# Operands of a linear recurrence and of windowed attention: loads that are issued earlier, from a pool of their own

## The chip, the cores and the metric

The kernel runs on one core of a Trainium2 chip as one program. The core has five instruction streams: TensorE (PE, with its weight loads shown as PEld), VectorE (DVE), ScalarE (ACT), GpSimd (POOL) and SyncE (SP, which here does nothing but issue DMAs). The time is that of one execution on the device, in microseconds (us). Of the kernel before there are three timed runs: 4224.21, 4231.0 and 4253.31, median 4231.0. One more execution was profiled.

## The reference, cut to what matters

One inference step of a two-layer backbone over 1280 tokens (256 of a prompt, 1024 latent ones), width 1024, all in float32. Layer 0 mixes by a gated DeltaNet and a short convolution, layer 1 by windowed attention and RWKV-7 side by side; a squared-ReLU MLP follows each. The change is in layer 1:

```python
def rwkv7_mixer(x, rw, s0_f, s0_b):
    x = token_shift_bi(x, mu)
    r, k, v, wl, al, gl = split_cols(x, RWKV_SPLITS)
    w_log = -softplus(-(w0 + einsum(tanh(wl), w_up))) - 0.5      # per direction
    decay = exp(-exp(w_log)); a = sigmoid(a0 + einsum(al, a_up)); gate = sigmoid(gl) @ g_up
    kk = l2norm(k * k_k); k2 = k * (1 + (a - 1) * k_a)
    y2, s2 = vmap(rwkv7_scan)(forward and reversed r, decay, k2, v, kk, a, states)
    y = y2[0] + y2[1][:, ::-1]
    y = groupnorm(y) * ln_w + ln_b
    bonus = sum(r * (k2_fwd + k2_bwd) * r_k) * v                 # over a head
    return (y + bonus) * gate, ...

def odd_mixer_latent(h, w_in, w_out, ...):
    q, k, v, x_rw = odd_project(h, w_in)
    att = attend_latent(rope_2d(q), rope_2d(k), v, ck, cv, sink) # 128-token blocks: 3 local blocks + 512 cached keys
    rwo = rwkv7_mixer(x_rw, rw, ...)
    return concat([att, rwo]) @ w_out
```

RWKV has 8 heads of 64. Two heads fill the 128 partitions, so there are four pairs b, each run in two directions d.

## The kernel before, in words

Every dense product is done in three matmuls: an activation and a weight are each split into a high and a low part (`split`, line 245: the high part by ACT on line 247, the low part by POOL on line 251), and high x high, high x low and low x high are added up in PSUM (line 275 for the projections; line 1283 for those that run later, beside the recurrence). A weight is loaded as `raw` by SP (`load_w`, line 263), then split into `whl`.

The Tile framework chooses each engine's order of instructions ahead of time, by a simulated timeline, and puts semaphores where one engine needs another. On each engine the order is then fixed: an instruction that waits holds up everything behind it, DMA issues on SP's queue included. Buffers come from pools; a tile that takes a place in SBUF over from another has to wait for its last reader.

Layer 1's mixer (`odd_mixer`) runs so:

1. The end of layer 0's MLP, then the norm. Three weight columns are asked for ahead (`ahead`, line 1086). x is written out to DRAM by `spill_x` (line 126).
2. Projections: q, k, v, the low-rank inputs (`sp_l`), and the first pair's r, k, kk (`sp_r`) and v. Results go to DRAM (`sp_...`).
3. The recurrence and attention. Eight units (b, d). `prep` builds a unit's operands in five groups of 256 tokens: loads rkk (line 1550) and lin (line 1553), multiplies lin with the pair's `ups` (loaded on line 1541, used on line 1557), and goes on to the arrays AR, BK and Gm. `recur` runs the unit's recurrence. Beside units 0 and 1 the r, k, v projections of pairs 1 to 3 run (line 1283, weights from a pool of its own). From unit 2 on attention runs beside it: `begin` of a 128-token block loads its keys kS (line 1393), used on line 1426. When both directions of a pair are done, `finish` makes five parts out of it: for each, r and the two k2 rows are loaded into vg (line 1814), added (POOL, line 1816) and multiplied (DVE, line 1817), then v and g are loaded into two of the same three places (lines 1819, 1820), and PE multiplies on lines 1855 and 1860. The last pair's finish is cut in two (`ahead`, lines 1873 and 1874, and `rest`).

Arrays AR of a group live in a pool of 8 buffers, to which `rmore` adds 3 from unit 2 on.

Of the kernel before, what the change touches and what calls it, by code (L numbers as in the profile page):

```python
# [18 lines left out]
P = 128  # L19
# [37 lines left out]
def gram_masks():  # L57

    m = np.zeros((P, 2, 2, P), np.float32)
    j, i = np.arange(64)[:, None], np.arange(64)[None, :]  # L60
    for d in range(2):
        past = (j < i) if d == 0 else (j > i)
        half = np.concatenate([past | (j == i), past], 1)
        m[:, d] = np.concatenate([half, half], 0)[:, None, :]
    return m
# [20 lines left out]
def tile_kernel(ctx, tc, I, O):  # L86
# [996 lines left out]
    def odd_mixer(xt, hs, hes, xes, wes):  # L1083
        wi = I["od_w_in"][0]

        ahead = [load_w(w_cols(wi, 768 + j * P)) for j in (12, 13, 14)]
# [135 lines left out]


# [82 lines left out]
        with ExitStack() as es:  # L1306
            prep, recur, finish = rwkv(es, sp_r, sp_v, sp_t, sp_l, sp_g, sp_k2)
# [21 lines left out]
            for u, (b, d) in enumerate(units):  # L1329
                cur = nxt  # L1330
                start = pace["cum"]
                recur(b, d, cur)
                if u == 2:
                    ed.close()
                    items = attention(es, sp_q, sp_k, sp_c, vtok_dram)
                    state["more"] = pool(es, "rmore", 3)
                if u + 1 < len(units):
                    nxt = prep(*units[u + 1])
                if u < 2:
                    slot, work = work[:per], work[per:]  # L1340
                else:
                    if u == 2:
                        per = iter((26,26,24,24,24, len(items)))
                    n = next(per)
                    slot, items = items[:n], items[n:]
                if u == 7:
                    pre, last = finish(b)
                    slot = [f for k, f in enumerate(slot) for f in ([f, pre.pop(0)] if k % 4 == 3 and pre else [f])] + pre
                    pace["used"] = max(pace["used"], start)
                k0 = len(slot) // 3  # L1350
                for k, f in enumerate(slot):
                    if ends and k >= k0 and (k - k0) * 5 // (len(slot) - k0) > 4 - len(ends):
                        ends.pop(0)()
                    f()
                while ends:
                    ends.pop(0)()
                if d == 1 and b < 3:
                    ends = finish(b)
            for f in last:
                f()  # L1360
        pace["on"] = False

    def attention(es, sp_q, sp_k, sp_c, vtok_dram):
# [145 lines left out]
    def rwkv(es, sp_r, sp_v, sp_t, sp_l, sp_g, sp_k2):  # L1509
# [6 lines left out]
        gmask = rc.tile([P, 2, 2, P], F32, name="gmask")  # L1516
        SY.dma_start(out=gmask, in_=I["cgm"].rearrange("p (d h q) -> p d h q", d=2, h=2))
# [15 lines left out]
        def prep(b, d):  # L1533

            if d == 0:
                ups = tp.tile([P, 3, P], F32, tag="ups", name="ups", bufs=2)
                for i, src in enumerate((I["rwkv_w_up"].rearrange("e d r c -> (e d r) c"),
                                         I["rwkv_a_up"].rearrange("e d r c -> (e d r) c"), I["rwkv_g_up"][0])):  # L1540
                    SY.dma_start(out=ups[:, i], in_=src[:, b * P:(b + 1) * P])
                live["ups", b] = ups
            ups = live["ups", b]
            pc = sp.tile([P, NC], F32, tag="pc", name="pc", bufs=3)
            order = [4, 0, 8, 12, 16] if d == 0 else [16, 0, 12, 8, 4]
            grp = {}
            for c0 in order:
                t0, sl = 64 * c0, slice(64 * c0, 64 * c0 + 256)
                rkk = tp.tile([P, 3, 256], F32, tag="rkk", name="rkk", bufs=2)
                SY.dma_start(out=rkk, in_=sp_r[b][:, :, sl])  # L1550
                r, k, kk = (rkk[:, i].rearrange("p (c q) -> p c q", q=64) for i in range(3))
                lin = tp.tile([P, 2, 256], F32, tag="lin", name="lin", bufs=1)
                SY.dma_start(out=lin[hr[d]], in_=sp_l.rearrange("x p t -> p x t")[hr[d], :, sl])
# [30 lines left out]
                g = state["more"] if state["more"] and turn[0] % 11 in (9, 10, 0) else gp  # L1584
# [9 lines left out]
                for h in range(2):  # L1594
                    ps = ps_t("pp")
                    for c in range(4):
# [3 lines left out]
                                    in1=gmask[:, d, h:h + 1].to_broadcast([P, 4, P]), op=ALU.mult)  # L1600
# [34 lines left out]
        def recur(b, d, unit):  # L1635
# [4 lines left out]
            for s in range(2):  # L1640
                SH[s] = tp.tile([P, 4, 64], F32, tag="SH", name="SH", bufs=4)
                if s == 0:
                    G.memset(SH[s][:, 0], 0.0)
                else:
                    raw = sp.tile([P, 64], F32, tag="sraw", name="sraw", bufs=2)
                    SY.dma_start(out=raw, in_=I[("state_rwkv_fwd", "state_rwkv_bwd")[d]][0, 0, 2 * b:2 * b + 2].rearrange(
                        "h v k -> (h v) k"))
# [158 lines left out]
        def finish(b):  # L1806
# [15 lines left out]
            def head_norm(Yt):  # L1822
# [5 lines left out]
                y2 = tp.tile([P, 4, 64], F32, tag="y2", name="y2", bufs=1)  # L1828
# [17 lines left out]
            def part(c0):  # L1846
                Yt = live.pop(("Y", b, c0 // 4))
                vg = tp.tile([P, 3, 256], F32, tag="vg", name="vg", bufs=1)
                steps = bonus(c0, vg)
                next(steps)  # L1850
                head_norm(Yt)
                next(steps, None)
# [3 lines left out]
                yT = tp.tile([P, 256], F32, tag="yT", name="yT", bufs=1)  # L1856
                affine(yT, ps)
                V.tensor_tensor(out=vg[:, 0], in0=vg[:, 0], in1=ps[:, 256:], op=ALU.mult)
                pg = ps_t("pa")
                PE.matmul(pg[:, :256], ups[:, 2, :], vg[:, 2], start=True, stop=True)  # L1860
                G.tensor_tensor(out=yT, in0=yT, in1=vg[:, 0], op=ALU.add)
# [6 lines left out]
            def ahead(c0):  # L1868
                vg = tp.tile([P, 3, 256], F32, tag="vg", name="vg", bufs=1)
                for _ in bonus(c0, vg):  # L1870
                    pass
                ps = ps_t("pa")
                paced(PE.matmul(ps[:, 256:], C["bd"], vg[:, 1], start=True, stop=True), 0.5)
                paced(PE.matmul(ps[:, :256], ups[:, 2, :], vg[:, 2], start=True, stop=True), 0.5)
                V.tensor_tensor(out=vg[:, 0], in0=vg[:, 0], in1=ps[:, 256:], op=ALU.mult)
# [3 lines left out]
            def rest(c0):  # L1879
# [3 lines left out]
                eg = tp.tile([P, 4, 3, 64] if tg == "BK" else [P, 3, 256], F32, tag=tg, name="eg", bufs=1 if tg == "vg" else 2)  # L1883
# [3 lines left out]
                head_norm(Yt)  # L1887
# [8 lines left out]
            if b < 3:  # L1896
                return [lambda c0=c0: part(c0) for c0 in order]
            return [lambda c0=c0: ahead(c0) for c0 in order], [lambda c0=c0: rest(c0) for c0 in order]
# [127 lines left out]
```

## Time and profile before

| | us |
|---|---|
| three timed runs, median | 4231.0 |
| the profiled execution | 4228.77 |
| its span, from first to last instruction | 4226.4 |
| PE busy | 3917.9 (93%) |
| DVE busy | 2285.1 (54%) |
| POOL busy | 1304.5 (31%) |
| ACT busy | 1287.8 (30%) |
| mean granted TensorE clock | 0.952 |

By the timeline, layer 0's MLP ends at 1860.8, the projections at 2065.1, and the recurrence with attention at 3164. "Idle before" or "waited for" says what released an engine after it had stood idle. [...]

### The profile page before, as it was taken

Reading aid. Unit: us, or ns where it says so; the run is one execution under the profiler, and the core shown is the slowest. Engines: PE = TensorE matmul, PEld = TensorE weight load, DVE = VectorE, ACT = ScalarE, POOL = GpSimd, SP = SyncE. Lnnn points to the kernel's source line nnn. Section 1 sums busy time; section 2 is a strip of 40 time slices with the busy share of each in tenths; the row PEclk is TensorE's granted clock in tenths of the full one; section 3 lists DMA queues with packets and bytes.
Section 4 is the critical chain, followed back from the end, with each engine's and each line's share of the span. In section 5 each row is a group of like instructions: output and inputs, shape, how many; then the busy total and the mean of one; then the engine's idle time right before and its main releaser. Section 6 shows DMA issues by size and latency. Waiting matters only on the chain. (4 is left out here: it accounts for less than half of the span.)

```text
span 4226.4 us, 68798 instructions
## 1 busy us (share of the span) xinstructions
PE 3917.9 (93%) x27295; PEld 3217.3 (76%) x27295; DVE 2285.1 (54%) x4800; ACT 1287.8 (30%) x2728; POOL 1304.5 (31%) x1140
## 2 busy tenths in 40 slices
PE   6989899999999999989889889899769899999999
PEld 4777778787888888878667667677658788888887
DVE  5567656554556665563365567777542533333335
ACT  4454543233111111143222234344231311111112
POOL 3354442233232222333432221322122423232232
PEclk8989999999999999999989799999889999999999
DMA  6333332431222222134565433333242111111111
GB/s 217 90 93 97 92 95 79 139 130 45 65 75 76 75 80 78 56 134 155 159 209 171 131 98 79 90 100 86 58 137 97 30 40 40 41 40 36 35 41 60
DMA packets 438656, 385.52 MB, mean 91 GB/s; under 512 B 125620, under 2 KB 375103, under 8 KB 438207
## 3 DMA queue, kind: packets, MB, share of 16 engines
q1 hardware_dynamic: 410352, 324.88, 26.0%
q10 hardware_dynamic: 27983, 56.24, 4.0%
q8 instruction: 215, 3.52, 0.3%
q14 instruction: 106, 0.87, 0.1%
HBM read 291.62 MB, written 89.39 MB: 90 GB/s over the span
## 5 line engine op out<-in xcount | busy, mean ns | idle before, releaser
L275 PE MATMUL pd<-hhi,whl 128*128 128x512 f32 (+1 forms) x5376 | 1531.9, 364 | 34.8 <-ACT hhi L247 13.5
L275 PEld LDWEIGHTS pd<-hhi,whl 128*128 128x128 f32 x5376 | 973.7, 192 | 195.2 <-ACT hhi L247 14.4
L275 PE MATMUL pd<-hlo,whl 128*128 128x512 f32 (+1 forms) x2688 | 980.2, 365 | 22.8 <-DVE hlo L460 11.8
L517 DVE SCALAR_TENSOR_TENSOR x<-pm,mods,x 128x512 f32<-128x512 f32 (+1 forms) x768 | 503.9, 660 | 720.7 <-PE pm L516 719.3
L251 POOL TENSOR_TENSOR whl<-raw,whl 128x1024 fp32r<-128x1024 f32 (+1 forms) x202 | 472.3, 2349 | 575.0 <-ACT whl L247 575.0
L275 PEld LDWEIGHTS pd<-hlo,whl 128*128 128x128 f32 x2688 | 516.0, 192 | 110.6 <-DVE hlo L460 17.4
L514 PE MATMUL pm<-hh,whl 128*128 128x512 f32 (+1 forms) x1536 | 546.1, 356 | 0.0
L515 PE MATMUL pm<-hl,whl 128*128 128x512 f32 (+1 forms) x1536 | 544.6, 355 | 0.0
L516 PE MATMUL pm<-hh,whl 128*128 128x512 f32 (+1 forms) x1536 | 543.5, 354 | 0.0
L503 ACT ACTIVATE t<-pd 128x512 f32<-128x512 f32 (+1 forms) x192 | 101.3, 528 | 1322.9 <-PE pd L275 1322.9
L251 POOL TENSOR_TENSOR hl<-t,hh 128x512 fp32r<-128x512 f32 (+1 forms) x192 | 216.2, 1127 | 855.3 <-DVE hh L249 855.3
L514 PEld LDWEIGHTS pm<-hh,whl 128*128 128x128 f32 x1536 | 289.1, 188 | 44.3
L515 PEld LDWEIGHTS pm<-hl,whl 128*128 128x128 f32 x1536 | 289.5, 189 | 42.7
L516 PEld LDWEIGHTS pm<-hh,whl 128*128 128x128 f32 x1536 | 289.7, 189 | 42.3
L249 DVE CAST hh<-t 128x512 fp32r<-128x512 f32 (+1 forms) x192 | 134.9, 703 | 193.6 <-ACT t L504 193.6
L247 ACT ACTIVATE whl<-raw 128x1024 fp32r<-128x1024 f32 (+1 forms) x202 | 201.4, 1015 | 124.9 <-PE pm L516 54.2
L366 POOL TENSOR_TENSOR acc<-acc,modw 128x512 f32<-128x512 f32 x112 | 150.5, 1344 | 140.4 <-ACT modw L362 106.6
L354 DVE SCALAR_TENSOR_TENSOR acc<-modw,scp,acc 128x512 f32<-128x512 f32 x168 | 162.9, 969 | 0.0
L362 ACT ACTIVATE modw<-modw,scp 128x256 f32<-128x256 f32 x224 | 112.6, 506 | 86.8 <-DMA modw<-in_mod_w_dram 83.7
L1283 PE MATMUL pa<-hst,whl 128*128 128x512 f32 (+1 forms) x432 | 125.2, 390 | 9.6 <-DMA hst<-sp_h 8.8
L425 ACT ACTIVATE sq<-x 128x512 f32<-128x512 f32 (+1 forms) x120 | 66.2, 559 | 165.4 <-DVE x L1934 49.8
L284 PE MATMUL pd<-hhi,whl 128*128 128x512 f32 (+1 forms) x384 | 109.3, 363 | 2.1 <-DVE xr L1026 1.2
(402 smaller groups left out, 5972.9 us busy)
## 6 DMA issues: line engine op xcount, KB each, us to landing
raw<-in_mlp_w_dram SPq DMA_DIRECT2D x128, 512.0 KB, 3.9
modw<-in_mod_w_dram SPq DMA_DIRECT2D x128, 256.0 KB, 3.0
hst<-sp_h ACTq DMA_DIRECT2D x48, 512.0 KB, 4.4
modw<-in_mod_w_dram SPq DMA_DIRECT2D x128, 128.0 KB, 2.2
rkk<-sp_r SPq DMA_DIRECT2D x40, 384.0 KB, 4.2
raw<-in_ev_w_in_dram SPq DMA_DIRECT2D x28, 512.0 KB, 3.8
x_dram<-x SPq DMA_DIRECT2D x16, 640.0 KB, 6.7
sp_i<-cv SPq DMA_DIRECT2D x12, 640.0 KB, 3.4
```

Of the source, the lines that this page charges most:

```text
L247: A.activation(out=hi, in_=src, func=AF.Copy)
L249: V.tensor_copy(out=hi, in_=src)
L251: G.tensor_tensor(out=lo, in0=src, in1=hi.bitcast(F32), op=ALU.subtract)
L275: paced(PE.matmul(ps[:, :N], w, x[:, t0:t0 + N], start=(n + i == 0), stop=(n == KB - 1 and i == 2)), N / 2400)
L354: bi = V.scalar_tensor_tensor(out=acc[:, s], in0=w, scalar=scp[:, kb, s:s + 1], in1=acc[:, s], op0=ALU.mult, op1=ALU.add)
L362: bi = A.activation(out=dst[:, s], in_=w[:, 0], func=AF.Copy, scale=scp[:, kb, s:s + 1])
L366: G.tensor_tensor(out=acc, in0=acc, in1=w, op=ALU.add)
L514: PE.matmul(ps[:, :N], wh, hh[:, b, :N], start=(b == 0), stop=False)
L515: PE.matmul(ps[:, :N], wh, hl[:, b, :N], start=False, stop=False)
L516: PE.matmul(ps[:, :N], wl, hh[:, b, :N], start=False, stop=(b == 1))
L517: state["evict"] = V.scalar_tensor_tensor(out=xt[db][:, t0:t0 + N], in0=ps[:, :N], scalar=gate[:, db, s:s + 1], in1=xt[db][:, t0:t0 + N], ...
L1283: burst([(lambda w_=w_, i=i, w=w, h=h: PE.matmul(st["ps"][w_][:, :N], st["w"][w_][:, w, kb, :], x[:, h, :N], start=(kb + i == 0), stop=(kb ...
```

## The change

It does six things. (a) At the start of the mixer the weight pools are closed, a pool `rin` is opened, and the weight pools are opened again behind it, at other addresses; ups, rkk and lin live in `rin`, and the first unit's first operands are loaded ahead of the recurrence stage, beside the projections. (b) The mask gmask is halved. (c) The incoming state of a unit is loaded in `prep`, no more in `recur`. (d) Keys kS have two buffers. (e) A finish part has five places in place of three (r, k2, k2, v, g), in a pool of two buffers; all five are loaded together, one part ahead; the separate tiles y2 and yT are gone. (f) `rmore` has 2 buffers in place of 3. No arithmetic changes.

```diff
     def odd_mixer(xt, hs, hes, xes, wes):
+        wes.close()
+        ri = ExitStack()
+        rin = pool(ri, "rin", 1)
+        open_w(wes, 3, 4)
         ahead = [load_w(w_cols(wi, 768 + j * P)) for j in (12, 13, 14)]
...
                     A.dma_start(out=sp_h[kb, :, i], in_=hs[kb][i].bitcast(F32))
+            unit0 = operands(rin, 0, 0, sp_r, sp_l)
...
-                    state["more"] = pool(es, "rmore", 3)
+                    state["more"] = pool(es, "rmore", 2)
+                    state["ends"] = pool(es, "rends", 2)
...
+    def operands(rin, b, d, sp_r, sp_l):
+        hd = slice(64 * d, 64 * d + 64)
+        ups = None
+        if d == 0:
+            ups = rin.tile([P, 3, P], F32, tag="ups", name="ups", bufs=2)
...
+        def group(c0):
+            sl = slice(64 * c0, 64 * c0 + 256)
+            rkk = rin.tile([P, 3, 256], F32, tag="rkk", name="rkk", bufs=2)
+            SY.dma_start(out=rkk, in_=sp_r[b][:, :, sl])
+            lin = rin.tile([P, 2, 256], F32, tag="lin", name="lin", bufs=1)
+            SY.dma_start(out=lin[hd], in_=sp_l.rearrange("x p t -> p x t")[hd, :, sl])
+            return rkk, lin
+        return ups, group, {4: group(4)} if (b, d) == (0, 0) else {}
...
-                kS = ap.tile([P, 4, 3 * P], F32R, tag="kS", name="kS", bufs=1)
+                kS = ap.tile([P, 4, 3 * P], F32R, tag="kS", name="kS", bufs=2)
...
+            raw = sp.tile([P, 64], F32, tag="sraw", name="sraw", bufs=2)
+            SY.dma_start(out=raw, in_=...)            # moved from recur into prep
+            live["raw", b, d] = raw
...
-                g = state["more"] if state["more"] and turn[0] % 11 in (9, 10, 0) else gp
+                g = state["more"] if state["more"] and turn[0] % 10 in (9, 0) else gp
...
-            def bonus(c0, vg):
+            def loads(c0):
                 sl = slice(64 * c0, 64 * c0 + 256)
-                for i, src in enumerate((sp_r[b][:, 0, sl], sp_k2[b % 2, 0][:, sl], sp_k2[b % 2, 1][:, sl])):
+                vg = state["ends"].tile([P, 5, 256], F32, tag="vg", name="vg")
+                for i, src in enumerate((sp_r[b][:, 0, sl], sp_k2[b % 2, 0][:, sl], sp_k2[b % 2, 1][:, sl], sp_v[b][:, sl],
+                                         sp_g[:, sl])):
                     SY.dma_start(out=vg[:, i], in_=src)
-                yield
+                return vg
+            here = {}
+            def operands_of(k):
+                for n in range(k, min(k + 2, 5)):
+                    if n not in here:
+                        here[n] = loads(order[n])
+                return here.pop(k)
+            def bonus(vg):
                 G.tensor_tensor(out=vg[:, 1], in0=vg[:, 1], in1=vg[:, 2], op=ALU.add)
...
-                SY.dma_start(out=vg[:, 0], in_=sp_v[b][:, sl])
-                SY.dma_start(out=vg[:, 2], in_=sp_g[:, sl])
```

How that moves instructions. First SP's queue at the end of layer 0's MLP; `raw<-in_mlp_w_dram` are the MLP's last weights, `raw<-in_od_w_in_dram` the mixer's first, `x_dram<-x` the spills. Before:

```order
L263 DMA raw<-in_mlp_w_dram 128x1024 [waits DMAHW2_49,Pool_49]
L263 DMA raw<-in_od_w_in_dram 128x8x128 [waits DMAHW7_49,DMAHW4_49,Pool_49]
...
L263 DMA raw<-in_od_w_in_dram 128x8x128 [waits DMAHW3_49,DMAHW0_49,Pool_49]
L126 DMA x_dram<-x 128x1280 [waits DVE_49] x5
```

and with the change:

```order
L263 DMA raw<-in_mlp_w_dram 128x1024 [waits DMAHW2_49,Pool_49]
L1378 DMA ups<-in_rwkv_w_up_dram 128x128 [waits DMAHW7_49,DMAHW6_49,Pool_49]
...
L126 DMA x_dram<-x 128x1280 [waits DMAHW1_49,DVE_49]
L263 DMA raw<-in_od_w_in_dram 128x8x128 [waits DMAHW2_49,PE_49]
L263 DMA raw<-in_od_w_in_dram 128x8x128 [waits DMAHW3_49,PE_49]
L263 DMA raw<-in_od_w_in_dram 128x8x128 [waits DMAHW4_49]
L126 DMA x_dram<-x 128x1280 [waits DMAHW5_49,DVE_49]
```

Five loads of the mixer's first weights stood ahead of the spills; now three stand behind the first five spills, and the first two of them wait for PE.

Second, SP's queue where the recurrence stage begins; `sp_k<-k` writes the first group's k2 out and waits for POOL, which makes it. Before:

```order
L263 DMA raw<-in_od_w_in_dram 128x4x128 [waits DMAHW0_49,PE_49]
L1541 DMA ups<-in_rwkv_w_up_dram 128x128 [waits DMAHW2_49,DVE_49,Pool_49]
...
L1550 DMA rkk<-sp_r 128x3x256 [waits DMAHW3_49]
L1553 DMA lin<-sp_l 64x2x256 [waits DMAHW4_49]
L1550 DMA rkk<-sp_r 128x3x256 [waits DMAHW5_49]
L263 DMA raw<-in_od_w_in_dram 128x4x128 [waits DMAHW6_49]
L263 DMA raw<-in_od_w_in_dram 128x4x128 [waits DMAHW7_49,Pool_49]
```

and with the change:

```order
L1571 DMA sraw<-in_state_rwkv_fwd_dram 128x64 [waits DMAHW1_49,PE_49]
L263 DMA raw<-in_od_w_in_dram 128x4x128 [waits DMAHW3_49,PE_49]
L263 DMA raw<-in_od_w_in_dram 128x4x128 [waits DMAHW5_49]
...
L1385 DMA lin<-sp_l 64x2x256 [waits DMAHW3_49,PE_49]
L1607 DMA sp_k_16325<-k_17822 128x256 [waits DMAHW4_49,Pool_49]
L1685 DMA VS<-sp_t 64x4x64 [waits DMAHW5_49]
L263 DMA raw<-in_od_w_in_dram 128x4x128 [waits DMAHW6_49,Pool_49]
```

The first group's operands are gone from this place (they stand among the projections' stores), two weight loads stand at its head, and the third stands behind the store of the first k2.

Third, SP's queue beside unit 2, at the second block's keys and a finish part. Before:

```order
L1819 DMA vg<-sp_v 128x256 [waits DMAHW4_49,DVE_49]
L1820 DMA vg<-sp_g 128x256 [waits DMAHW6_49,DMAHW5_49,Pool_49]
L1550 DMA rkk<-sp_r 128x3x256 [waits DVE_49,Pool_49]
L1393 DMA kS<-sp_k 64x4x384 [waits DMAHW7_49,PE_49]
L1393 DMA kS<-sp_k 64x4x384 [waits DMAHW0_49]
```

and the third block's keys with the change:

```order
L1841 DMA vg<-sp_v 128x256 [waits DMAHW4_49]
L1841 DMA vg<-sp_g 128x256 [waits DMAHW5_49]
L1438 DMA q<-sp_q 64x2x128 [waits DMAHW6_49,PE_49]
L1438 DMA q<-sp_q 64x2x128
L1421 DMA kS<-sp_k 64x4x384 [waits DMAHW0_49]
```

The loads of v and g wait for no arithmetic any more, and from the third block on the keys do not wait for PE to be done with the block before.

## Rows read from the trace of the kernel before

**Rows 1.** Windows: length, each engine's busy time, clock, DMA share, GB/s.
```profile
1860.00:1870.00 10.00, 4.85 (x19) 3.04 (x17) 10.00 (x13) 6.58 (x12) 8.37 (x5) 0.70 1.04 374
1860.00:1900.00 40.00, 27.14 (x99) 19.03 (x98) 29.59 (x47) 23.59 (x42) 18.43 (x20) 0.76 0.68 249
2050.00:2100.00 50.00, 34.99 (x184) 25.84 (x182) 14.01 (x23) 12.03 (x25) 22.69 (x33) 0.83 0.65 197
2100.00:3050.00 950.00, 846.21 (x9485) 648.50 (x9485) 639.50 (x1746) 347.80 (x891) 226.41 (x322) 0.90 0.43 116
```

**Rows 2.** Waits of PE, 2060 to 3180: total us, times, longest.
```profile
PE pa L1426 <- DMA kS<-sp_k: 14.2, 8, 3.1
PE pp L1557 <- DMA lin<-sp_l: 13.0, 1, 13.0
...
PE pa L1873 <- DVE vg L1817: 5.8, 4, 2.2
PE pa L1855 <- DVE vg L1817: 5.7, 3, 4.0
PE pa L1456 <- DVE vg L1858: 5.3, 2, 4.7
...
PE pi L1650 <- DMA sraw<-in_state_rwkv_fwd_dram: 2.1, 1, 2.1
PE pa L1860 <- DVE vg L1858: 2.1, 2, 1.9
...
PE pa L1456 <- DVE yT L1862: 1.2, 1, 1.2
```

**Rows 3.** Timeline of PE, start of the recurrence stage: start, duration, instruction.
```profile
2064.84 0.27 PE L275 MATMUL pd<-hhi,whl 128*128 128x256 f32 x1
2078.13 1.19 PE L1557 MATMUL pp<-lin,ups 64*128 64x256 f32 x2 [13.01 <-DMA lin<-sp_l]
...
2083.96 2.57 PE L1283 MATMUL pa<-hst,whl 128*128 128x512 f32 x6
...
2094.64 0.70 PE L1557 MATMUL pp<-lin,ups 64*128 64x256 f32 x2
```

**Rows 4.** Timeline of SP's issues, same place.
```profile
2064.09 0.38 SPq L263 DMA_DIRECT2D raw<-in_od_w_in_dram  x1
...
2075.50 1.16 SPq L263 DMA_DIRECT2D raw<-in_od_w_in_dram  x2
...
2084.01 1.09 SPq L263 DMA_DIRECT2D raw<-in_od_w_in_dram  x2
2085.20 0.46 SPq L1580 DMA_DIRECT2D sp_k<-k  x1
```

**Rows 5.** DMA issues by what they move: count, KB each, median us to landing.
```profile
x_dram<-x SPq DMA_DIRECT2D x16, 640.0 KB, 6.7
...
raw<-in_od_w_in_dram SPq DMA_DIRECT2D x8, 512.0 KB, 3.9
```

**Rows 6.** Waits of DVE, 2420 to 3060.
```profile
DVE vg L1817 <- POOL vg L1816: 27.4, 11, 5.1
```

**Rows 7.** Waits of POOL, 2420 to 3060.
```profile
POOL vg L1816 <- DMA vg<-sp_k: 35.1, 9, 5.0
POOL AR L1587 <- PE pc L1775: 33.0, 11, 9.3
```

**Rows 8.** Timeline of SP's issues, end of layer 0's MLP.
```profile
1789.89 55.98 SPq L263 DMA_DIRECT2D raw<-in_od_w_in_dram  x5
1855.27 4.28 SPq L126 DMA_DIRECT2D x_dram<-x  x5
```

**Rows 9.** Timeline of PE, first matmul of the projections.
```profile
1860.82 0.39 PE L275 MATMUL pd<-hhi,whl 128*128 128x512 f32 x1
```

**Rows 10.** Timeline of POOL, same norm: a weight's low part, the norm's last low part.
```profile
1862.36 5.14 POOL L251 TENSOR_TENSOR whl<-raw,whl 128x1024 fp32r<-128x1024 f32 x2 [0.16 <-ACT whl L247]
...
1897.60 0.73 POOL L251 TENSOR_TENSOR hlo<-t,hhi 128x256 fp32r<-128x256 f32 x1 [3.42 <-ACT hhi L247]
```

More of the change, by code (lines that the diff above doesn't have):

```diff
@@ L1533, in prep @@
         def prep(b, d):
+            ups, group, first = unit0 if (b, d) == (0, 0) else operands(rin, b, d, sp_r, sp_l)
             if d == 0:
[L1538 to L1541, printed above, removed]
                 live["ups", b] = ups
             ups = live["ups", b]
+            raw = sp.tile([P, 64], F32, tag="sraw", name="sraw", bufs=2)
+            SY.dma_start(out=raw, in_=I[("state_rwkv_fwd", "state_rwkv_bwd")[d]][0, 0, 2 * b:2 * b + 2].rearrange(
+                "h v k -> (h v) k"))
+            live["raw", b, d] = raw
             pc = sp.tile([P, NC], F32, tag="pc", name="pc", bufs=3)
@@ L1548, in prep @@
                 t0, sl = 64 * c0, slice(64 * c0, 64 * c0 + 256)
-                rkk = tp.tile([P, 3, 256], F32, tag="rkk", name="rkk", bufs=2)
-                SY.dma_start(out=rkk, in_=sp_r[b][:, :, sl])
+                rkk, lin = first.pop(c0, None) or group(c0)
                 r, k, kk = (rkk[:, i].rearrange("p (c q) -> p c q", q=64) for i in range(3))
-                lin = tp.tile([P, 2, 256], F32, tag="lin", name="lin", bufs=1)
-                SY.dma_start(out=lin[hr[d]], in_=sp_l.rearrange("x p t -> p x t")[hr[d], :, sl])
                 ps = ps_t("pp")
@@ L1844, in affine, with part @@
                              bias=vec["ln_b"][:, b:b + 1])
-            def part(c0):
+            def part(k):
+                vg = operands_of(k)
+                c0 = order[k]
                 Yt = live.pop(("Y", b, c0 // 4))
[L1848 to L1852, printed above, removed]
+                bonus(vg)
+                head_norm(Yt, vg[:, 2])
                 ps = ps_t("pa")
@@ L1855, in part @@
                 PE.matmul(ps[:, 256:], C["bd"], vg[:, 1], start=True, stop=True)
-                yT = tp.tile([P, 256], F32, tag="yT", name="yT", bufs=1)
+                yT = vg[:, 0]
                 affine(yT, ps)
-                V.tensor_tensor(out=vg[:, 0], in0=vg[:, 0], in1=ps[:, 256:], op=ALU.mult)
+                V.tensor_tensor(out=vg[:, 3], in0=vg[:, 3], in1=ps[:, 256:], op=ALU.mult)
                 pg = ps_t("pa")
-                PE.matmul(pg[:, :256], ups[:, 2, :], vg[:, 2], start=True, stop=True)
-                G.tensor_tensor(out=yT, in0=yT, in1=vg[:, 0], op=ALU.add)
+                PE.matmul(pg[:, :256], ups[:, 2, :], vg[:, 4], start=True, stop=True)
+                G.tensor_tensor(out=yT, in0=yT, in1=vg[:, 3], op=ALU.add)
                 V.tensor_tensor(out=yT, in0=yT, in1=pg[:, :256], op=ALU.mult)
@@ L1865, in finish, with ahead @@
             order = (16, 0, 12, 8, 4)
[L1868 to L1871, printed above, removed]
+            def ahead(k):
+                vg = operands_of(k)
+                c0 = order[k]
+                bonus(vg)
                 ps = ps_t("pa")
                 paced(PE.matmul(ps[:, 256:], C["bd"], vg[:, 1], start=True, stop=True), 0.5)
-                paced(PE.matmul(ps[:, :256], ups[:, 2, :], vg[:, 2], start=True, stop=True), 0.5)
-                V.tensor_tensor(out=vg[:, 0], in0=vg[:, 0], in1=ps[:, 256:], op=ALU.mult)
+                paced(PE.matmul(ps[:, :256], ups[:, 2, :], vg[:, 4], start=True, stop=True), 0.5)
+                V.tensor_tensor(out=vg[:, 0], in0=vg[:, 3], in1=ps[:, 256:], op=ALU.mult)
                 A.activation(out=vg[:, 1], in_=ps[:, :256], func=AF.Copy)
@@ L1882, in rest @@
                 tg = EG[order.index(c0)]
-                eg = tp.tile([P, 4, 3, 64] if tg == "BK" else [P, 3, 256], F32, tag=tg, name="eg", bufs=1 if tg == "vg" else 2)
+                pl, shape = {"rkk": (rin, [P, 3, 256]), "BK": (tp, [P, 4, 3, 64]), "vg": (state["ends"], [P, 5, 256])}[tg]
+                eg = pl.tile(shape, F32, tag=tg, name="eg", bufs=2)
                 if tg == "BK":
@@ L1896, in finish @@
             if b < 3:
-                return [lambda c0=c0: part(c0) for c0 in order]
-            return [lambda c0=c0: ahead(c0) for c0 in order], [lambda c0=c0: rest(c0) for c0 in order]
+                return [lambda k=k: part(k) for k in range(5)]
+            return [lambda k=k: ahead(k) for k in range(5)], [lambda c0=c0: rest(c0) for c0 in order]
         return prep, recur, finish
```

28 lines of the change are left out of this document (15 added, 13 removed).

## The prediction, made before the changed kernel had run

> **What bounds the kernel now.** I began with the windows by stage, since the change touches layer 1's mixer only. In the recurrence stage from 2100 to 3050 TensorE is busy 846 us of 950, DVE 640 [rows 1]: PE sets the pace, DVE at 67% stands close behind, and no transfer limit shows (DMA share 0.43). So a DMA only matters where PE stands still for it. The second view is therefore PE's waits from 2060 to 3180 [rows 2]. Those that name a tile of this change are: the first low-rank input, once, 13.0; attention's keys, 8 times, 14.2; the finish parts 5.8 + 5.7 + 5.3 + 2.1 + 1.2 = 20.1; the incoming state, 2.1. Together 49.4 us. That is the ceiling at the level of waits, 1.2% of the kernel; the rest of PE's waits belongs to arithmetic that is not touched. Third, the timelines at the two places where SP's queue is reordered: the start of the recurrence stage [rows 3, 4] and the end of layer 0's MLP [rows 8 to 10].
>
> **Part by part.** *Start of the recurrence stage.* PE's last projection matmul ends at 2064.84 + 0.27 = 2065.11, the first low-rank product starts at 2078.13 [rows 3]: 13.0 us in which its operands are read back. The change issues those loads among the projections' stores, so this product can follow at once: up to -13.0. How much is kept is decided by the next matmuls, which need weights. Before, the second and third weight pieces were issued at 2075.50 and about 2076.1, and the third one's products ran at 2083.96; the fourth was issued at 2084.01 [rows 3, 4]. With the change the first two are issued together where one was, near 2064, but the third stands on SP behind the store of the first k2. That store came 2085.20 - 2078.13 = 7.1 us after the first product [rows 3, 4]; 7.1 after 2065.2 is 2072.3. So the third piece is issued some 3.5 us earlier than before, and the fourth, a little later in the queue at about 2075 to 2077, 7 to 9 us earlier. Between 3.5 and 9, and with ends of 0 and -13, I take **-7**.
>
> *Keys.* With two buffers and an issue most of a block earlier, the load no longer waits for the last matmul on the old keys: the whole 14.2 us can go, at least nothing does. *Finish parts.* POOL stood 35.1 us for the k2 rows [rows 7], DVE 27.4 us for POOL behind that [rows 6], and PE 20.1 for DVE [rows 2]. With all five loads one part ahead the first of these goes, and with it a part of the others; what is left is that an add, a multiply and a normalisation still follow one another on three engines. I take half, 10 of 20.1 (ends 0 and 20.1). Of the 14.2 + 10 = 24 I expect half to be kept, since what PE does next in most of these places needs DVE, whose 67% is an average over the same stretch: **-12** (ends 0 and -34.3). DVE's and POOL's own waits are not added: idle time there costs only through PE. *State in.* Its load comes a unit earlier: -2.1 to 0, I take **-1**. The halved mask saves a load beside other work and leaves the multiply's shape alone: 0, and had its load been in PE's way, a wait on it would stand among PE's waits.
>
> *Group buffers.* POOL's first write of a group already stands 33.0 us for a buffer of the unit before [rows 7]. With 10 buffers in place of 11 units 6 and 7 get theirs one group later. PE stands idle 104 us of the 950 [rows 1], so mostly there is room; ends 0 and +9.3, the longest such wait, I take **+2**.
>
> *Weights of the projections.* Here something gets worse. Before, five loads of the mixer's weights were issued from 1789.89 on, under the MLP [rows 8]. Now they take their places at new addresses, behind the first five spills of x, issued from 1855.27 to 1859.55 [rows 8]. A 512 KB weight takes 3.9 us to land [rows 5]; from about 1859.7 that is 1863.6 if the spills do not hold it up. If they do: 5 x 640 KB [rows 5] at 374 GB/s [rows 1] take 8.8 us, to 1864.1, and the weight lands about 1868. Then a split follows, a low part taking 2.6 (two in 5.14) [rows 10]. So the first projection matmul, at 1860.82 before [rows 9], comes between 1864.6 and 1869, that is 4 to 8 us later. What covers it is the norm: its last low part is made only at 1897.60 [rows 10], and in 1860 to 1900 PE is busy 27.1 of 40 us [rows 1], so 12.9 us are free. I take **+1** (ends 0 and +9).
>
> [...]
>
> Sum: -7 - 12 - 1 + 2 + 1 = **-17 us**. The profiled execution took 4228.8, which gives 4211.8. It stands 2.2 under the median of the three runs, 4231.0; measured from that median the forecast is **4214**.
>
> **The rivals.** *All waits are real gain, and the clock comes back too.* The granted clock was 0.83 in 2050 to 2100 [rows 1]; after the 13 us of rest two low-rank products took 1.19, and at 2094.64 the same two 0.70 [rows 3]. [...] For it: POOL and DVE stand 35 and 27 us in the finish chain, so that more than PE's own waits could loosen, and the mean clock of 0.90 in the stage leaves room. Against it: the third weight behind the k2 store, and DVE's own load.
>
> [...]
>
> *The waits change their names.* Keys and finish operands are there earlier, PE stops at the same places for DVE or ACT, and at the start it waits for the third weight: -8 to +6, near 4229. This is also the case in which the change does not do what it says, because the early loads stand in SP's queue behind a wait. For it: the third weight's place, and that the fixed orders of all five engines are newly drawn, by a simulation and not by the chip. Against it: on SP the key loads and the five loads of a part now wait for nothing that is late, from the third block on.
>
> *Slower: the projections' first weight.* If the norm gives no cover, because the two norm matmuls of the second token chunk now stand on PE behind the first matmul that needs the weight, the 4 to 8 us are paid in full, a third split of 2.6 falls among POOL's low parts of the norm, and part of the stretch from 1860 to 1900, already at clock 0.76 [rows 1], stays at the lower level: 8 + 2.6 and up to a quarter of 27 us, together +10 to +17. It decides once the first projection matmul comes later than about 1860.8 + 12.9 = 1873.7. With half the gains (-8.5) and all of the group buffers' 9.3 that is +11 to +18 net, near 4245.
>
> **How the numbers follow.** Forecast (-8 to -28): 0.48. All waits and clock (-28 to -60): 0.24, of which beyond -42: 0.13. Waits change their names (-8 to +6): 0.15. Slower: 0.13, of which beyond +42: 0.04, which takes an order of work that goes wrong at a place I do not see. A measurement of this kernel can tell about 1%, 42 us, from no change: faster by more 0.13, within 0.83, slower by more 0.04. The range: from -46 (leaving about 0.10 below) to +10 (leaving about 0.10 above): 4185 to 4241. The likeliest case alone would reach from 4203 to 4223.
>
> **What would show it.** In the profile of the changed kernel: no wait on lin near 2065, the first low-rank product within 2 us of the last projection matmul, and a wait for weight splits of some 5 us in its place. Keys: a sum under 3 in place of 14.2. PE's waits on finish tiles at about 10; POOL's wait on the k2 rows near 0. First projection matmul between 1864 and 1869, and the projections' end within 3 us of where it was. I am wrong if that end moves by over 8 us, if PE's waits on untouched arithmetic grow by what the others lose, or if the mean clock of the stage rises well above 0.90.

## The result, and the profile after

The changed kernel took 4189.93 us (median of 4 runs, 4185.28 to 4192.78), the kernel before 4235.43 (4 runs): ratio 0.9895, 95% interval 0.9872 to 0.9919, that is 44 us less (34 to 54). Its profiled execution took 4192.78, with a span of 4191.0. The forecast was 17 us less. The sign is right and the time lies inside the range, but the change was worth two and a half times what the sum said.

Windows of the changed kernel: first the projections, from the MLP's last matmul to the last projection matmul, then the recurrence and attention, from there to the first matmul of the output projection. Columns as in [rows 1].

```profile
1864.30:2075.40 211.10, 187.60 (x966) 155.58 (x966) 95.13 (x130) 71.47 (x122) 83.52 (x74) 0.94 0.48 166
2075.40:3129.07 1053.67, 938.45 (x10762) 720.94 (x10762) 702.46 (x1909) 392.82 (x1013) 263.16 (x376) 0.90 0.45 123
```

The same two stretches of the kernel before:

```profile
1861.00:2065.00 204.00, 189.15 (x966) 155.42 (x965) 87.49 (x129) 69.90 (x120) 77.52 (x72) 0.95 0.44 155
2065.11:3164.07 1098.96, 945.91 (x10763) 723.80 (x10762) 695.56 (x1909) 395.07 (x1013) 263.97 (x376) 0.89 0.43 120
```

The projections became 7 us longer, the recurrence stage 45.3 us shorter: PE is busy 7.5 us less (with the same matmuls) and idle 115.2 in place of 153.1. Everything outside of the two stretches is code that the change does not touch; layer 0's MLP ended 3.3 us later in the changed kernel's profiled execution, and the two profiled executions differ by 36.0 us where the medians differ by 44.

PE's waits in that stage of the changed kernel, the largest and all that still name a tile of the change over 1 us (total, times, longest), against [rows 2]:

```profile
PE pi L1747 <- ACT Gm L1721: 11.6, 8, 3.8
PE pa L1288 <- DMA hst<-sp_h: 10.8, 12, 2.3
PE pc L1775 <- DVE SH L1784: 8.4, 14, 1.2
...
PE pa L1454 <- DVE vg L1893: 3.1, 2, 2.5
...
PE pp L1584 <- DMA ups<-in_rwkv_w_up_dram: 1.4, 1, 1.4
PE pp L1584 <- DMA lin<-sp_l: 1.4, 1, 1.4
```

The key wait is gone, the finish tiles' waits on DVE fell from 20.1 to 4, the low-rank input from 13.0 to 2.8 with its weights. Summed over all rows, the waits that name the change's tiles ("named" from here on) went from 52.9 to 6.9, all others from 86.6 to 98.8. So of 46 us removed 12 came back under other names; PE's idle time, in which short gaps without a releaser count too, fell by 37.9.

One sign of the prediction did not come: POOL's wait on the k2 rows was to be near 0. It is 28.1 where it was 35.1 [rows 7]; DVE's wait for POOL behind it fell from 27.4 [rows 6] to 14.4 (changed kernel, 2405 to 3035):

```profile
POOL vg L1854 <- DMA vg<-sp_k: 28.1, 7, 8.8
DVE vg L1855 <- POOL vg L1854: 14.4, 9, 3.8
```

The stage has two parts. Up to attention's first matmul the change touches only the first operands, the mask and the state's load; keys, finish parts and the additional group buffers are used from there on. PE's windows of the two parts, first before, then with the change:

```profile
2065.11:2418.40 353.29, 299.04 (x2397) 231.30 (x2397) 189.15 (x419) 95.82 (x214) 102.67 (x144) 0.84 0.63 183
2418.40:3164.07 745.67, 646.88 (x8366) 492.51 (x8366) 506.41 (x1490) 299.25 (x799) 161.29 (x232) 0.92 0.34 90
```
```profile
2075.40:2423.70 348.30, 301.47 (x2462) 231.11 (x2462) 195.54 (x429) 97.92 (x220) 106.88 (x147) 0.86 0.63 184
2423.70:3129.07 705.37, 636.99 (x8300) 489.83 (x8300) 506.92 (x1480) 294.91 (x793) 156.28 (x229) 0.92 0.36 93
```

The first part is 5.0 us shorter (7.4 less idle time, 2.4 more busy time), the second 40.3 (30.4 less idle time, 9.9 less busy time).

The start of the two stages, PE's timeline of the changed kernel (answers to [rows 3, 9]):

```profile
1873.44 0.80 PE L275 MATMUL pd<-hhi,whl 128*128 128x512 f32 x1 [9.15 <-ACT whl L247]
...
2075.93 0.70 PE L1584 MATMUL pp<-lin,ups 64*128 64x256 f32 x2 [0.53 <-ACT qf L1267]
...
2081.30 3.62 PE L1288 MATMUL pa<-hst,whl 128*128 128x512 f32 x6 [2.59 <-ACT ip L1599]
```

and SP's, same kernel (answers to [rows 4, 8]):

```profile
1858.58 4.28 SPq L126 DMA_DIRECT2D x_dram<-x  x5
1862.95 6.28 SPq L263 DMA_DIRECT2D raw<-in_od_w_in_dram  x3
...
2074.72 0.94 SPq L263 DMA_DIRECT2D raw<-in_od_w_in_dram  x2
...
2083.30 0.32 SPq L1607 DMA_DIRECT2D sp_k<-k  x1
2085.79 0.38 SPq L263 DMA_DIRECT2D raw<-in_od_w_in_dram  x1
...
2087.56 0.55 SPq L263 DMA_DIRECT2D raw<-in_od_w_in_dram  x1
```

The first projection weight is asked for behind the spills, and its matmul starts 9.2 us after the MLP's last one. The first low-rank product follows the last projection matmul within a microsecond, at a granted clock of 1.00 and not 0.50 (0.70 us, not 1.19 as in [rows 3]). But the third weight piece is issued 10.4 us after the projections' end, against 11.0 before: behind the k2 store, as said, and 2.5 us behind even that. The fourth is issued 12.2 us after that end, against 18.9.

### The profile page after: what moved, and what is told of

Its sections match the earlier page's. It is cut to its first block, busy times and chain, and to the rows that moved or that the text cites. A ratio compares the mean times of both kernels' runs of the same rounds, so it can differ in the third digit from the quotient of the medians.

```text
span 4191.0 us, 68743 instructions
## 1 busy us (share of the span) xinstructions
PE 3910.3 (93%) x27295; PEld 3216.7 (77%) x27295; DVE 2296.8 (55%) x4800; ACT 1284.9 (31%) x2728; POOL 1303.7 (31%) x1140
## 5 line engine op out<-in xcount | busy, mean ns | idle before, releaser
L275 PE MATMUL pd<-hlo,whl 128*128 128x512 f32 (+1 forms) x2688 | 978.9, 364 | 13.1 <-POOL hlo L251 6.7
L514 PEld LDWEIGHTS pm<-hh,whl 128*128 128x128 f32 x1536 | 289.0, 188 | 44.3
```

Source lines behind the costliest of these rows:

```text
L275: paced(PE.matmul(ps[:, :N], w, x[:, t0:t0 + N], start=(n + i == 0), stop=(n == KB - 1 and i == 2)), N / 2400)
L514: PE.matmul(ps[:, :N], wh, hh[:, b, :N], start=(b == 0), stop=False)
```

## The experiments

I divided the change into parts, and then, since the parts did not add up, drew the same kernels again. "Draw" stands for the order of instructions that the scheduler makes from a program: a number of the pacing (how much dense work it places beside a given length of the recurrence, 1.2 in all kernels above) moved to 1.25 or 1.15 leaves work, buffers and loads alone and moves thousands of lines of PE's order. It is not a neutral number, since it also moves dense work from one part of the stage to the other. Ratios are to the kernel before on the same chip; 0.01 is 42 us.

**One part undone.** One key buffer (e1):

```diff
-                kS = ap.tile([P, 4, 3 * P], F32R, tag="kS", name="kS", bufs=2)
+                kS = ap.tile([P, 4, 3 * P], F32R, tag="kS", name="kS", bufs=1)
```

> The changed kernel with one key buffer again, all else kept. The changed kernel took 44 us less than the one before, where I forecast 17. Theory A (the named waits were real time and nearly all of them was kept): PE's wait for keys comes back at 10 to 14 us and the time is 10 to 14 above the changed kernel's, near 4203. Theory B (half of such a wait is taken back by the next one, as I forecast): waits come back at 10 to 14, the time rises by 5 to 7, near 4196. Theory C (the gain is mostly a newly drawn order of instructions, not these waits): the time moves by some amount that PE's key wait does not explain, either under 3 or over 20.

Ratio 0.9953 (0.9936 to 0.9971), -20 us: 24 dearer than the changed kernel. PE's wait for keys in it:

```profile
PE pa L1454 <- DMA kS<-sp_k: 4.7, 3, 2.0
```

Only 4.7 came back, so neither A nor B explains the 24. C stands: PE's waits on untouched tiles, summed over the stage, were 117, not 99.

One buffer for the finish parts, no part ahead (e2; the last pair's `rest` takes one tile from the same pool, and that has one buffer then, too):

```diff
-                    state["ends"] = pool(es, "rends", 2)
+                    state["ends"] = pool(es, "rends", 1)
...
-                for n in range(k, min(k + 2, 5)):
+                for n in range(k, k + 1):
```

> The changed kernel with one buffer for the finish parts and no part loaded ahead; the five loads of a part still go out together, into five places. Theory A: PE's waits behind the finish tiles return from about 4 us to 15 to 20, the time rises by 11 to 16, near 4203. Theory B: waits the same, time up 5 to 8. Theory D (the finish chain was worth more than PE's own waits on it, since POOL stood 35 and DVE 27 us in it): the time rises by 20 to 30, near 4215. Theory C: it moves by an amount that these waits do not explain.

0.9977 (0.9960 to 0.9994), -10 us: 34 dearer, somewhat over D's number. The recurrence stage of this kernel:

```profile
2071.65:3170.71 1099.06, 957.55 (x10762) 737.53 (x10762) 705.57 (x1909) 392.64 (x1013) 262.69 (x376) 0.87 0.43 118
```

Busy 957.6 against 938.5: 19 of the 45 us by which the stage is longer are the same matmuls at a mean granted clock of 0.87 against 0.90, and its waits on finish tiles are 9.5. This profiled execution was 11 us longer than the median of its twelve, so a part of the 19 is the execution's own. The number alone would have spoken for D; the profile does not.

Weight pools left where they were, the new pool opened as the projections end (e3):

```diff
-        wes.close()
-        ri = ExitStack()
-        rin = pool(ri, "rin", 1)
-        open_w(wes, 3, 4)
         ahead = [load_w(w_cols(wi, 768 + j * P)) for j in (12, 13, 14)]
...
         set_ps(pc=1, pp=2, pi=1, pa=3, po=1)
+        ri = ExitStack()
+        rin = pool(ri, "rin", 1)
+        unit0 = operands(rin, 0, 0, sp_r, sp_l)
```

> The changed kernel with the projections' weight pools left where they were in the kernel before; the pool for the first operands takes their place only as the projections end, and the first unit's operands are loaded then, still ahead of the recurrence stage. Theory A: the first projection matmul follows the MLP's last at once (9.2 us of wait in the changed kernel), the projections take 204 us and not 211, and the time falls by 6 to 8 below the changed kernel's, near 4183; the first low-rank product still starts within 3 us of the last projection matmul. Rival: those 7 us were made up later by the changed kernel anyway, or the first operands are now late again (a wait of 5 to 13 us), and the time is the same within 3.

0.9911 (0.9894 to 0.9928). Its first projection matmul, on PE's timeline:

```profile
1863.29 0.28 PE L516 MATMUL pm<-hh,whl 128*128 128x256 f32 x1
1863.41 0.39 PE L275 MATMUL pd<-hhi,whl 128*128 128x512 f32 x1
```

It follows the MLP at once, and the projections take 203.4 us, so the 7 us are the price of the new addresses; in all five kernels that have them the first projection matmul comes 9.2 us after the MLP's last. The first operands come early all the same. Yet the recurrence stage took 1065.8 in place of 1053.7, and by their intervals the two times cannot be told apart. The first half of A holds, the second doesn't.

**One part added to the kernel before.**

```diff
-    kS ... bufs=1      state["more"] = pool(es, "rmore", 3)
+    kS ... bufs=2      state["more"] = pool(es, "rmore", 2)   # e4: keys
+    finish parts of the change, rmore 2, kS one buffer        # e5: ends
+    both, and the halved mask                                 # e6
```

> The kernel before with two key buffers and, for the room, two in place of three of the additional group buffers; nothing else. Theory A: PE's wait for keys falls from 14.2 to under 3, the time falls by 10 to 14 less what the group buffer costs (0 to 4), so 7 to 13 below the kernel before. Theory B: by 3 to 6. Theory C: no such relation; a redrawn order could give anything from -25 to +25. If the group buffer is dear, the time rises by up to 9.

e4: 0.9989 (0.9974 to 1.0003). The key wait went to 0, and nothing was gained: waits on untouched tiles rose from 86.6 to 128, and PE stood idle 158 us in the stage, not 153.

> The kernel before with the finish parts of the change (five places, two buffers, loads one part ahead) and, for the room, two in place of three additional group buffers; one key buffer, nothing else. So far, against the kernel before: all parts together -44 us, all but the key buffer -20, all but the finish parts -10, the keys alone -2. Theory D (the finish parts carry the gain): 15 to 25 below the kernel before, near 4215; PE's waits behind finish tiles fall from 23 to under 6. Theory C (each redrawn order wins or loses some 10 to 20 us by itself, and a removed wait is in part taken over by waits on arithmetic): anything from -30 to +10, and PE's waits on untouched arithmetic in the stage, 87 us before and 99 in the changed kernel, decide: about 120 of them if the gain is small.

e5: 0.9989 (0.9974 to 1.0004), with 0.7 of waits on finish tiles, 115 on untouched ones and 152 of idle time. Theory D falls.

> As the one before, with two key buffers too, and the halved mask, which gives the room: the kernel before with keys and finish parts of the change, but with the first operands where they were. If the parts add up: -2 of the keys alone and the gain of the finish parts alone. Theory E (the two need each other: either wait alone, left in, stops PE at the same block): -30 to -40, near 4200, though each alone gives under half. Theory C: no fixed relation; PE's waits on untouched arithmetic again decide. The wait of 13 on the first low-rank input stays.

e6: 1.0001 (0.9987 to 1.0015). E falls as well, for this order. The key wait is 0, the finish tiles' is 5.2 in place of 22.8 (with their DMAs), and the time is the same.

**The state's load**, for which I had forecast -1. First put back into recur, on e3; then moved into prep, on e6 and on the kernel before alone:

```diff
+            raw = sp.tile([P, 64], F32, tag="sraw", name="sraw", bufs=2)   # in prep
+            SY.dma_start(out=raw, in_=...)
+            live["raw", b, d] = raw
...
-                    raw = sp.tile([P, 64], F32, tag="sraw", name="sraw", bufs=2)   # in recur
-                    SY.dma_start(out=raw, in_=...)
+                    raw = live.pop(("raw", b, d))
```

> The version with the weight pools left in place (36 us below the kernel before), with one part undone: the incoming state is loaded in recur again. Keys and finish parts alone, without a pool for the first operands and without this move, gave nothing (4240 against 4238). Theory F (the state's load, moved ahead into prep, is what lets the rest count): the time goes back to 4230 to 4240. Theory G (the operands' own pool, read a stage earlier, is): the time stays within 12 of that version's 4199. Theory C (draws of order): anywhere between.

> Keys, finish parts and halved mask on the kernel before (4240), with the state's load moved into prep as well; the operands stay in their old pool, so the 13 us wait for the first low-rank input stays. Theory F: falls by 20 to 35, to 4205 to 4220 (what is left to 4199 is the 13 us). Theory G: within 10 of 4240. Theory C: anywhere from 4205 to 4250.

e9 0.9952 (0.9935 to 0.9969), e10 0.9891 (0.9865 to 0.9917). On e6 the move is worth 47 us, on e3 17. Both lie outside of the bands of F and G: e9, at 4213, between them, and e10, at 4188, below F's. Taken alone, e10 looks like the cause found.

> The kernel before with the state's load moved into prep, nothing else. Theory F (the state's place in the program frees the recurrence by itself): 20 to 45 below the kernel before, near 4205. Theory H (the move only counts once keys and finish parts are out of the way, and they only with it): within 10 of 4236. Theory C (draws of order): anything in -25 to +20.

e13: 0.9977 (0.9956 to 0.9999), -10 us: by itself the move gives little, which is H's number, or C's.

**The same kernels, drawn again.**

```diff
-            grant["ratio"] = 1.2
+            grant["ratio"] = 1.25      # or 1.15
```

> The changed kernel with one number of the pacing moved from 1.2 to 1.25: how much dense work the scheduler places beside a given length of the recurrence. All buffers, loads and arithmetic are as in the changed kernel; some 4600 lines of PE's order move. Theory A or E: the same within 8 us of the changed kernel's 4190. Theory C: the changed kernel drew a lucky order, and this one lies 8 to 25 above, near 4205, with PE's waits on the change's own tiles still under 10 and those on untouched arithmetic 110 or more in place of 99.

> The kernel before with the same number moved from 1.2 to 1.25, nothing else. Theory A or E: the same within 8 us of 4235. Theory C: off by 8 to 25 either way, and rather slower, if the kernel before was itself the best of several orders that were tried.

> Keys, finish parts and halved mask on the kernel before (4240), pacing number 1.25 in place of 1.2. It gives a second draw of that group. Theories F and G: within 12 of 4240, and over 4225. Theory C: it may fall to 4210 or rise to 4255.

> The version with the weight pools left in place (4199), pacing number 1.25 in place of 1.2: a third draw of the group that has the operands' own pool, beside 4190 and 4213. Theories F and G: 4190 to 4215. Theory C: may reach 4230.

> Keys, finish parts, halved mask and the state's load in prep on the kernel before (4188 with pacing 1.2), drawn again with pacing 1.25. Theories F and H: 4180 to 4205. Theory C: the 4188 was a lucky draw, and this lies at 4210 to 4240.

> The same group, drawn a third time with pacing 1.15. Theories F and H: 4180 to 4205. Theory C: 4210 to 4240.

> Keys, finish parts and halved mask on the kernel before, without the state's move (4240 and 4235 with pacing 1.2 and 1.25), drawn a third time with pacing 1.15. Theories F and H: 4228 to 4250. Theory C: may lie at 4190 to 4215.

> The kernel before, drawn a third time (pacing 1.15; 4236 with 1.2, 4251 with 1.25). Theory C, as the runs so far have it: single draws of one and the same set of buffers scatter by some 20 us either way around their mean; for the kernel before without the change 4225 to 4260. If it came to 4200 or less, the scatter alone would reach as far as the whole change, and nothing but the mean over draws could be said of the change at all.

> The changed kernel, drawn a third time (4190 with 1.2, 4213 with 1.25). Theory C: 4185 to 4225. With it there are three draws of either side at the same three pacing numbers; I expect the mean of the three differences at -25 to -45, that is the change is a gain beyond the draw, and the 44 us of the first pair is partly the draw's.

C's forecasts came true for e7, e8, e14, e16 and e18; e11 and e12 came as F and G had it, which C allowed as well; e15 (4209) lay between, and e17 (4220) below all that C allowed. Ratios by the pacing number, e-numbers in brackets:

| | 1.2 | 1.25 | 1.15 | mean |
|---|---|---|---|---|
| kernel before | 1 | 1.0026 (8) | 0.9962 (17) | 0.9996 |
| + keys and ends | 1.0001 (6) | 0.9994 (11) | 0.9886 (16) | 0.9960 |
| + keys, ends, state | 0.9891 (10) | 0.9951 (14) | 0.9923 (15) | 0.9922 |
| whole change, weights not moved | 0.9911 (3) | 0.9949 (12) | | 0.9930 |
| whole change | 0.9895 | 0.9941 (7) | 0.9913 (18) | 0.9916 |

One line scatters by up to 0.0115, 49 us, more than the whole change. None of these kernels beats the changed one beyond its interval. e16 has neither the state's move nor the pool and is as fast as the changed kernel; e14 has e10's parts and is 25 us slower than e10. So a difference of 10 to 30 us between two of these kernels, one draw each, tells nothing of the part in which they differ: e1, e2, e9 and e10 are explained by that as well as by any mechanism, and F is not shown. What does hold: at each of the three numbers the changed kernel is faster than the one before, by 1.05, 0.85 and 0.49%, 0.80% or 34 us on the mean. Three differences that far apart fix their mean to some 30 us either way and no better.

Where the scatter lies is seen in the recurrence stage of e6 and of e16, which differ in the pacing number alone; and of e10. First e6:

```profile
2069.55:3184.60 1115.05, 964.29 (x10763) 739.96 (x10762) 704.78 (x1909) 391.73 (x1013) 264.98 (x376) 0.87 0.43 118
```

then e16:

```profile
2069.78:3127.45 1057.67, 929.34 (x10763) 712.74 (x10763) 693.04 (x1909) 392.14 (x1013) 260.06 (x376) 0.91 0.45 124
```

and e10:

```profile
2067.22:3121.73 1054.51, 920.89 (x10763) 706.40 (x10762) 699.68 (x1909) 392.06 (x1013) 257.25 (x376) 0.91 0.45 125
```

The same 10763 matmuls keep PE busy for 964, 929 and 921 us, at a mean clock of 0.87, 0.91 and 0.91. Of the 57 us between e6 and e16, 35 are that, and 22 are idle time (150.8 against 128.3).

Means over three draws, split so. In us, "named" being PE's waits on the change's own tiles:

| mean of three draws | stage | PE busy | PE idle | named |
|---|---|---|---|---|
| kernel before | 1099.5 | 942.4 | 157.1 | 43.9 |
| + keys and ends | 1090.9 | 946.7 | 144.2 | 18.9 |
| + keys, ends, state | 1071.6 | 932.7 | 138.9 | 18.2 |
| whole change | 1062.6 | 940.9 | 121.7 | 5.0 |

From the first line to the last, named waits fall by 38.9 and idle time by 35.4, while busy time is the same within 2. From the first to the second line it is not so: named waits fall by 25.0 and idle time by 12.9, half of that. The same means by the two parts of the stage:

| mean of three draws | idle, first part | named | idle, second part | named |
|---|---|---|---|---|
| kernel before | 58.8 | 13.3 | 98.3 | 30.7 |
| + keys and ends | 58.5 | 13.6 | 85.6 | 5.4 |
| + keys, ends, state | 54.7 | 13.1 | 84.2 | 5.1 |
| whole change | 49.5 | 0 | 72.3 | 5.0 |

The first part shows what the early operands do. At pacing 1.2 PE is idle there 50.5 to 55.7 us in the six kernels that load them late (before, e4, e5, e6, e10, e13; mean 54.1) and 43.7 to 47.9 in the five that load them early (changed, e1, e2, e3, e9; mean 46.3): 7.8 us, with no overlap. The second part scatters far more: 89.1 to 107.0 in the three draws of the kernel before, 68.4 to 95.1 in the twelve kernels that have both two key buffers and the new finish parts in two buffers (mean 82.2; the last three lines of the table, e3, e9 and e12). On the mean these twelve have 25 us less of named waits than the kernel before and 16 less of idle time, two thirds; single ones have 3 to 30 less. e3 and e12, which have all that the second part uses of the change, are idle there for 83.0 and 88.1 us and not for 72.3. So even a mean over three draws is uncertain by some 10 us, and why the whole change does best there stays open.

The changed kernel's two other draws show it row by row, e7 and e18:

```profile
2066.70:3132.78 1066.08, 941.89 (x10764) 723.61 (x10763) 695.03 (x1909) 392.76 (x1013) 258.21 (x376) 0.90 0.44 122
```
```profile
2071.30:3139.42 1068.12, 942.34 (x10764) 721.96 (x10763) 699.35 (x1909) 391.32 (x1013) 257.45 (x376) 0.90 0.44 122
```

against those of the kernel before, e8 and e17:

```profile
2061.40:3174.54 1113.14, 945.92 (x10764) 724.04 (x10763) 699.65 (x1909) 393.18 (x1013) 260.68 (x376) 0.89 0.43 118
```
```profile
2069.57:3156.09 1086.52, 935.44 (x10764) 717.49 (x10763) 699.80 (x1909) 395.60 (x1013) 260.71 (x376) 0.90 0.44 121
```

## Why the prediction was wrong

**The step that failed** is "of the 14.2 + 10 = 24 I expect half to be kept", the term of -12, with the halving of the finish waits before it. In this pair the second part of the stage, where keys and finish parts are used, lost 33.0 us of named waits (39.9 to 6.9), 30.4 of idle time and 9.9 of busy time: 40 us, where the sum had -12 and +2. The waits were the right ones and went nearly in full, at the finish parts from 20.1 to 4 where I took half. That the next wait takes half back was wrong for this pair, where it took 2.6 of 33.0. Another share cannot be put in its place as a rule: over three draws the kernels with keys and finish parts alone kept 12.7 of 25.3, the whole change 26.0 of 25.7. A DVE busy for 67% of the stage was my reason; it is at 67% still (702.5 of 1053.7), so that share does not tell the cases apart. The rival "all waits are real gain" has this pair's -44 in its band (-28 to -60), but e4 to e6 got rid of the waits on keys and finish tiles, singly and together, and gained nothing, so the match is owed in part to this order. Its clock came in part only: 0.84 to 0.86 in the first part, 0.89 to 0.90 in the stage; how much clock a shorter wait gives back, no run here shows.

**Start of the stage**, -7 forecast: right in size, -5.0 in this pair's first part (7.4 less idle time), and 7.8 less idle time between the five kernels with early operands and the six without. It was right partly by luck, since the course was another. The low-rank product came 12.5 us earlier; the third weight, to which I had given 3.5, came 0.6 earlier and the fourth 6.7 (7 to 9 forecast). SP's order said where the third stands, behind the k2 store, and I had not counted its further wait there. The first unit's first result was 196.2 us behind the projections' end before and 196.4 after, its last one 293.0 and 289.0, so the unit itself gained some 4 us by its end; that the rest of the gain lies in the dense work beside it is not shown by a row.

**Weights of the projections**, +1 forecast with ends 0 and 9: +7 measured, in the trace and by e3's 203.4 against 211.1. The first matmul came at 9.2 after the MLP's end (4 to 8 forecast), since the split on ACT stood in its queue behind the norm's own work until 1872.34, as ACT's timeline of the changed kernel has it:

```profile
1871.82 0.61 ACT L247 ACTIVATE hhi<-t 128x512 fp32r<-128x512 f32 x1
1872.34 1.04 ACT L247 ACTIVATE whl<-raw 128x1024 fp32r<-128x1024 f32 x1
```

ACT had worked without a gap from 1869.99 on, so whether the weight had landed before its turn came isn't seen. The low part's 2.6, which I had put on this path, was not on it: the first matmul waited for the high part alone, 1.04 on ACT. The norm was no cover: PE's idle time in the stage was 15 before and 23.5 after, because its later waits did not shrink (14.8 before, 14.3 after without the 9.2). The projections' end moved by 10.3 us, of which 3.3 are the MLP's later end. Whether the weights' transfers had to wait for those of the spills, as the later of my two times had it, is not shown: the third of the three weights landed 8.0 us after its issue, against a median of 3.9 in [rows 5]; the first one's landing is not in the trace.

**Group buffers**, +2: POOL's wait for them more than doubled against [rows 7]; the changed kernel, 2405 to 3035:

```profile
POOL AR L1614 <- PE pc L1800: 77.1, 19, 9.8
```

But PE's own wait for POOL's AR in the stage is 0.7, so 0 would have been nearer.

**State**, -1: not settled. Its own wait was 2.1 and could give no more by itself. Two means of three draws, with and without the move, differ by 16 us, and a single draw scatters by as much.

**What was missing** is a term for the draw; I had it only as an argument for a rival with a chance of 0.15. Any of these edits makes the scheduler order five engines anew, and with the same buffers (keys and ends) the pacing number alone moved the time between 0.9886 and 1.0001. On the mean of three pairs 35 us of idle time less 7 at the projections are 28, with 34 measured; the six profiled executions themselves differ by 31, which accounts for half of the rest. The 44 of the first pair lie 10 above that mean, and in its two profiled executions PE is busy 7.5 us less in the stage, which does not return on the mean (1.5). How much of the 30 us of idle time in the second part is this draw's, and how much the change's, no run here separates. That the time still lay inside the range is owed to the range's width.

## What to carry to other kernels

Before believing that an edit's part did something, draw the same kernel twice or thrice with a number that changes the order and as little else as possible; where the draws scatter by as much as the effect, compare means. Better still, cut the stage at a fixed point of the program and compare PE's idle time there: in the short first part 8 us stood out clearly between eleven kernels, in the long second one three draws did not settle 12. How much of a removed wait is kept can't be read from one pair: here it was anything from nothing to all of it, two thirds on the mean of twelve kernels. And moving a pool to new addresses has a price where its first loads used to hide under the stage before, 7 us here.

## What the runs showed of the hardware

At the start of the recurrence stage the granted clock differs between the two kernels of this pair, as the wait does. Before the change PE had stood still for 13.0 us when the first low-rank product came, and the clock was 0.50; with the change that product came 0.5 us after the last projection matmul, and the clock was 1.00. First before, then after:

```profile
2078.00:2079.50 1.50, 1.37 (x3) 0.75 (x4) 0.00 (x0) 0.15 (x1) 0.00 (x0) 0.50 1.17 321
```
```profile
2075.50:2077.00 1.50, 0.96 (x6) 0.49 (x6) 0.76 (x2) 0.71 (x2) 0.85 (x12) 1.00 0.60 176
```

With the change the clock did not stay at 1.00 there: from 2081.30 to 2084.92, after 2.59 us without a matmul, it was 0.50. These are the two values that nearly all short windows show: from 2065 to 3169, in windows of 0.2 us, the clock was 1.00 or 0.50 in 5469 of 5520 before and in 5477 of 5520 with the change. The prediction's "lower level" is the 0.50.

Over a whole stage the clock is a part of the time that goes with the order of work: 921 to 964 us of busy time for the same 10763 matmuls, at granted clocks of 0.91 to 0.87. It is not the order alone: e2's twelve executions, of one program, ran from 4210 us at a mean clock of 0.954 to 4249 us at 0.944. What makes it fall at which places was not isolated here.
